# Fourier units of a hybrid GLA/FNet step: high and low data side by side in one moving operand

## The chip, the cores and the metric

The kernel runs on one core of a Trainium2 chip. Its engines work side by side, each through its own instructions in order: TensorE (PE; its weight loads are shown as PEld), VectorE (DVE), ScalarE (ACT), GpSimd (POOL) and SyncE (SP), which here issues the transfers. The metric is the device time of one execution in microseconds; the time given is the median of several runs.

## The reference

One layer of a diffusion backbone on 384 tokens (128 of context, 256 latent) of width 2048: modulation, a mixing sub-layer, a dense feed-forward sub-layer. The part that matters is the mixer's Fourier branch and the merge:

```python
fg = fo.astype(jnp.float32).reshape(bsz, t, FOURIER_GROUPS, FOURIER_GROUP_DIM)
f = jnp.fft.fft2(fg, axes=(1, 3), norm='ortho').real
...
gates = jax.nn.sigmoid(h @ lw['w_gate'] + lw['b_gate'])
g_a, g_b = jnp.split(gates, 2, axis=-1)
merged = g_a * (o @ lw['w_br_gla']) + g_b * (f @ lw['w_br_four'])
return merged @ lw['w_out'], s_f, s_b
```

All data are float32. Context and latent tokens are transformed separately, in 4 groups of 256 channels.

## The kernel before

**Precision and layout.** Activations lie transposed, channels on the 128 partitions and the 384 tokens in the free dimension. A float32 operand is kept as two float32r parts, high (the value rounded by a copy) and low (the difference), and a product is three products: high by high, high by low, low by high. `gemm` (L248) writes them in the order weight-high by data-high, weight-high by data-low, weight-low by data-high, each with its own weight load; PSUM sums them.

**The weight feed.** Weights come in tiles of 128 x 1024, in one fixed list `srcs`. `load` (L185) issues the next transfer from SP into one of two buffers `raw`. `split` (L205) makes the two parts: ACT casts `whi` (L218), DVE subtracts `wlo` (L219); there are four buffers of each. A tile of the Fourier projection is folded first (`fold`, L195): one addition and one subtraction on DVE (L199, L200) into the single buffer `ws`. `grab` (L239) takes the oldest finished tile and pushes the next one, so a tile is used three takes after its push. With `hold=True` the split of a folded tile is put off until `settle` (L228), which the unit calls at its end. PE, ACT, DVE and POOL run their instructions in the order in which the program writes them; SP is not in that list in this part, and its order is the framework's.

**The stage.** `dft` makes the transformed data: `eT` (cosine part) and `dT` (sine part), each four blocks of 128 channels by 194 columns. 194 is 65 + 129: of a real transform only half of the positions, and one more, are kept for context and latent tokens; the sum and the difference of the two parts give both halves. `pnr` holds one more row group (the Nyquist channels), multiplied by `wn`. Before the change the high parts of `eT` and `dT`, the low part of `eT` and `pnr` lie in one tile `edT` in the place C_lo, each block 194 columns (776 bytes) from the next, and the low part of `dT` is a tile `dlo` of its own.

**The order of the stage** is `mix_order` (L155): block o0, then for i = 1 to 7 the block o_i and the Fourier units b of 2i-2 and 2i-1; then a0, b14, a1, b15, a2 to a15. A block o is a projection with two weight tiles (48 products of 384 columns) whose result `gcol` (L967) turns into a gated, split `oT`: three transposes on PE, a SiLU on ACT, one DVE operation, a split. A block a is the GLA branch's projection (24 products of 384 columns), multiplied by its gate and added to what unit b of the same number has stored (L1018, L1019). `gate_of` (L950) loads the gate of a later block and applies the sigmoid on ACT. Pieces of another computation (`ada_rest`, on DVE) are interleaved at a fixed rate by blocks o and a.

**A Fourier unit** (`four`, L976) takes one folded tile, 512 columns for `eT` and 512 for `dT`, and makes 2 x 12 products of 194 columns and one with `wn` (L984) into one PSUM bank: the two halves of `pf`. ACT copies the second half to `fd` (L987), which has one buffer; DVE forms the 384 positions with two additions and two subtractions (L991, L992), multiplies by the gate (L995), SP stores the result to `four_d` (L996), and `settle` splits the held tile. PSUM has 3 buffers in the pool `psm` (where `pf` and the projections' results lie) and 5 in the pool `pss`.

Of the kernel before, what the change touches and what calls it, by code (L numbers as in the profile page):

```python
# [11 lines left out]
F32 = mybir.dt.float32  # L12
F32R = mybir.dt.float32r
# [7 lines left out]
P = 128  # L21
# [4 lines left out]
T = TC + TL  # L26
# [22 lines left out]
HT = HC + HL  # L49
# [47 lines left out]
def tile_step(ctx: ExitStack, tc: tile.TileContext, a, o):  # L97
    nc = tc.nc
    PE, ACT, DVE, POOL, SP = nc.tensor, nc.scalar, nc.vector, nc.gpsimd, nc.sync
# [3 lines left out]
    actp = ctx.enter_context(tc.tile_pool(name="actp", bufs=1))  # L103
# [124 lines left out]
    def settle():  # L228
        if half_done:
            half_done.pop()()  # L230

    def push(at=None, eng=DVE, hold=False):
        load()
        split(at, eng, hold)

    def take():
        return ready.pop(0)

    def grab(hold=False):  # L239
        w = take()  # L240
        push(hold=hold)
        return w
# [5 lines left out]
    def gemm(dst, w, x, kts, n=P, n0=0, k0=0, first=True, last=True):  # L248

        for k in range(kts):  # L250
            for j, (wi, xi) in enumerate(((0, 0), (0, 1), (1, 0))):
                PE.matmul(  # L252
                    dst, w[wi][:, k * n + n0 : k * n + n0 + P], x[xi][:, k0 + k, :],
                    start=first and k == 0 and j == 0, stop=last and k == kts - 1 and j == 2,
                )
# [21 lines left out]
    def split_act(hi, lo, src):  # L277
        ACT.copy(hi, src)
        DVE.tensor_sub(lo, src, hi.bitcast(F32))
# [29 lines left out]
    psm = ctx.enter_context(tc.tile_pool(name="psm", bufs=3, space=PSUM))  # L309
    pss = ctx.enter_context(tc.tile_pool(name="pss", bufs=5, space=PSUM))  # L310
    with ExitStack() as s:
# [95 lines left out]
        def xprod(u, kb, w):  # L407
            def mm():
                for j, (x_, w_) in enumerate(passes(w)):
                    PE.matmul(px, w_[:, u * P : (u + 1) * P], hT[x_][:, kb, :], start=j == 0, stop=j == 2)  # L410

            return mm, lambda dst=None: flush(xacc[u], kb == 0, dst)
# [127 lines left out]
        for t in range(3):  # L540
            vprod(KT - 1, prev[0], range(3), (t,))
            if t < XU:
                mm, fl = xprod(t, KT - 1, prev[1])
# [298 lines left out]
    with ExitStack() as s:  # L842
        pc = s.enter_context(tc.tile_pool(name="pc", bufs=1))
        fold_in.append(pc)
        b0 = C_CR
        cd = pc.tile([P, NC - b0], F32, name="cd")
        SP.dma_start(cd, a["consts"][:, b0:NC])
        oT = alloc_r("B", "o")

        cl = actp.tile([P, 13 * HT], F32R, tag="C_lo", name="edT").rearrange("p (n t) -> p n t", t=HT)  # L850
        eT, dT = (cl[:, 0:4], cl[:, 4:8]), (cl[:, 8:12], pc.tile([P, 4, HT], F32R, name="dlo"))
        pnr = cl[:, 12]
        fs = {}
        nyq = pc.tile([P, 3, P], F32, name="nyq")
        POOL.memset(nyq, 0.0)
# [2 lines left out]
        wn = pc.tile([P, D], F32R, name="wn")  # L858
        done = [0]

        def dft():


            def left(dst, stat, m):

                for lat, base, n in ((0, C_CT - b0, HC), (1, C_LT - b0, HL)):
                    for k in range(1 + lat):
                        c0 = base + (m * (1 + lat) + k) * n
                        PE.matmul(  # L869
                            dst[:, HC * lat : HC * lat + n], stat(lat + k), cd[:, c0 : c0 + n],  # L870
                            start=k == 0, stop=k == lat,
                        )

            for g in range(4):
                while done[0] < 2 * g + 2:
                    yield
                yield
                xc = pc.tile([P, 3, 2, 2, P], F32, tag="xc", name="xc")
                for t in range(3):
                    px = pss.tile([P, 257], F32, tag="side", name="px")  # L880
                    ts = slice(t * P, (t + 1) * P)
                    e, d = fs[g][:, 0, ts], fs[g][:, 1, ts]
                    PE.matmul(px, d, cd[:, 129:386], start=True, stop=False)  # L883
                    PE.matmul(px[:, 0:129], e, cd[:, 0:129], start=False, stop=True)

                    for m, c0 in enumerate((0, 129)):
                        ACT.copy(xc[:, t, m], px[:, c0 : c0 + P].unsqueeze(1).to_broadcast([P, 2, P]))
                    ACT.copy(nyq[:, t, g : g + 65 : 32], px[:, 128:129].to_broadcast([P, 3]))
                yield
                off = (P - 32 * g) % P  # L890
                rot = xc.rearrange("p t m r c -> p t m (r c)")
                for m, x in enumerate((eT, dT)):
                    pp = pss.tile([P, HT], F32, tag="side", name="pp")
                    left(pp, lambda k: rot[:, k, m, off : off + P], m)
                    split_act(x[0][:, g, :], x[1][:, g, :], pp)
                yield
            pn = pss.tile([P, HT], F32, tag="side", name="pn")
            left(pn, lambda k: nyq[:, k, :], 0)
            ACT.copy(pnr, pn)
            DVE.tensor_sub(pnr[64:96], pn[64:96], pnr[64:96].bitcast(F32))  # L900
            yield

        def nyq_weights():

            n = D // 2
            for h in range(2):
# [13 lines left out]
                yield  # L920

        df = dft()

        def side():
# [50 lines left out]

        def four(i):  # L976

            pf = psm.tile([P, 512], F32, tag="mm", name="pf")
            p = pf[:, 0 : 2 * HT].rearrange("p (m t) -> p m t", m=2)
            w = grab(hold=True)  # L980
            for m, x in enumerate((eT, dT)):
                gemm(p[:, m, :], [v[:, 512 * m : 512 * m + 512] for v in w], x, 4, last=m == 1)
                if m == 0:
                    PE.matmul(p[:, 0, :], wn[0:96, i * P : (i + 1) * P], pnr[0:96], start=False, stop=True)  # L984
            g, _ = gates.pop(("b", i))
            d = pc.tile([P, HT], F32, tag="fd", name="fd")
            ACT.copy(d, p[:, 1, :])  # L987
            y = pc.tile([P, T], F32, tag="yb", name="y", bufs=4)
            for lo, n, base in ((0, TC, 0), (TC, TL, HC)):
                h = n // 2  # L990
                DVE.tensor_add(y[:, lo : lo + h], p[:, 0, base : base + h], d[:, base : base + h])  # L991
                DVE.tensor_sub(  # L992
                    y[:, lo + h : lo + n], p[:, 0, base + h : base : -1], d[:, base + h : base : -1],
                )
            DVE.tensor_mul(y, y, g)  # L995
            SP.dma_start(four_d[i], y)  # L996
            settle()
# [3 lines left out]
        for b, i in mix_order:  # L1001
            if b == "o":
                if i == 1:
                    gate_of()
                proj(psm, hT, lambda p: gcol(p, i), sd)
                if i == 1:
                    gate_of()
                continue
            if b == "b":
                four(i)  # L1010
            else:
                if mT is None:
                    mT = alloc_A()
                    rate[0] = 0.15
                p = psm.tile([P, T], F32, tag="mm", name="pmm")
                gemm(p, grab(hold=True), oT, 8)
                g, y = gates.pop((b, i))
                DVE.tensor_mul(g, g, p)  # L1018
                DVE.tensor_add(y, y, g)  # L1019
                settle()  # L1020
                if late:
                    split_act(*late.pop())
                late.append((mT[0][:, i, :], mT[1][:, i, :], y))
                step(sd)
            gate_of()
# [6 lines left out]
    with ExitStack() as s:  # L1032
# [49 lines left out]
        for i in range(KT):  # L1082
            p = psm.tile([P, T], F32, tag="mm", name="pmm")
            for g in range(2):
                n = 2 * i + g - 2 * KT
                if n < -6:
                    w = grab()
                else:

                    w = take()  # L1090
# [132 lines left out]
        for k in range(KT + 1):  # L1223
# [9 lines left out]
            if k:  # L1233
                if k % 8 == 1:
                    hw = [take() for _ in range(HEAD)]
                for j, m in ((0, 0), (1, 0), (0, 1)):
                    for u in range(HEAD):
                        PE.matmul(  # L1238
                            hp[u], hw[u][j][:, ((k - 1) % 8) * P : ((k - 1) % 8 + 1) * P], h2[m][:, k - 1, :],
                            start=k == 1 and j == m == 0, stop=k == KT and m == 1,  # L1240
# [12 lines left out]
        pf = s.enter_context(tc.tile_pool(name="pf", bufs=1))  # L1253
# [75 lines left out]
        pairs = []  # L1329
# [75 lines left out]
        def grab2(kept=2):  # L1405
            w = take()
            while now:
                now.pop(0)()
            load_more(kept)
            split_next()  # L1410
            return w
# [52 lines left out]
        for u in range(HEAD):  # L1464
            kind, c, j = ffn_order[u]
            dst_of[kind](hp[u], c, j)
        n = 0
        for kind, c, j in ffn_order[HEAD:]:
            p = psm.tile([P, T], F32, tag="mm", name="pmm")
# [98 lines left out]
        for kind, c, i in steps:  # L1568
# [8 lines left out]
            if kind == "D":  # L1577
                w = grab2()
                n, kh = i // 2, i % 2
                if kh == 0:  # L1580
# [3 lines left out]
                    pool, tag = (pss, "side") if done % 2 or (c, n) == (NFC - 2, 3) else (psm, "mm")  # L1584
                    pd_tiles = [pool.tile([P, 512], F32, tag=tag, name="pdn") for _ in range(3)]
                    d_live[0] = 3
                h = hid_last if last_c else hid
# [27 lines left out]
            else:  # L1615
                if kind == "A" and i == 0:
                    banks(c)
                w = grab2()
# [18 lines left out]
        n = d_order[-1]  # L1637
# [144 lines left out]
```

## Time and profile before

| | |
|---|---|
| median of 3 runs | 1968.85 us (1968.83 to 1969.10) |
| the profiled execution | 1969.33 us, of which the span is 1967.6 us |
| granted TensorE clock | 0.999 |
| PE busy in the span | 99% |
| stage of the Fourier units (first to last product of a unit) | 598.66 to 705.1 us |
| products of the 16 units | 400, of 194 columns |
| DMA over the span | 380.08 MB, mean 193 GB/s |

How to read it. The page and the views give instructions by line, engine, operation and tile: `pf<-edT,whi` is a product that writes `pf` from `edT` and `whi`. In a timeline the columns are start (us), duration (us), engine, line, operation, tiles, shapes and the count of merged instructions; the brackets give the idle time of the engine before it and what released it. Products are pipelined, so the time from one start to the next, not the duration, is what a product costs. A row of the view by windows gives the window, its length, and for PE, PEld, DVE, ACT and POOL the busy time with the number of instructions, then the clock, the share of the DMA engines and GB/s. In the chain of waits a row is start, length, engine, tile, line and count. In the view of one tile three durations in ns (least, median, most) stand behind the count.

### The profile page before, as it was taken

Reading aid. Unit: us, or ns where it says so; the run is one execution under the profiler, and the core shown is the slowest. Engines: PE = TensorE matmul, PEld = TensorE weight load, DVE = VectorE, ACT = ScalarE, POOL = GpSimd, SP = SyncE. Lnnn points to the kernel's source line nnn. Section 1 sums busy time; section 2 is a strip of 40 time slices with the busy share of each in tenths; the row PEclk is TensorE's granted clock in tenths of the full one; section 3 lists DMA queues with packets and bytes.
Section 4 is the critical chain, followed back from the end, with each engine's and each line's share of the span. In section 5 each row is a group of like instructions: output and inputs, shape, how many; then the busy total and the mean of one; then the engine's idle time right before and its main releaser. Section 6 shows DMA issues by size and latency. Waiting matters only on the chain.

```text
span 1967.6 us, 27720 instructions
## 1 busy us (share of the span) xinstructions
PE 1951.9 (99%) x10704; PEld 1731.7 (88%) x10704; DVE 1620.2 (82%) x2043; ACT 905.7 (46%) x1265; POOL 32.2 (2%) x44
## 2 busy tenths in 40 slices
PE   8999999999999999999999999999999999999998
PEld 6779999999999999999988888888888888888886
DVE  5569788878767778877789998999898999887875
ACT  4233454544345645446454444444444444444444
POOL 0000000000000000004000000000000000000001
PEclk9999999999999999999999999999999999999999
DMA  9978677767755697655345445463636363626243
GB/s 388 372 257 275 211 255 238 234 218 246 238 183 182 197 312 222 196 171 203 119 136 186 149 140 162 154 188 118 193 127 205 100 209 103 208 75 193 75 161 128
DMA packets 189412, 380.08 MB, mean 193 GB/s; under 512 B 14172, under 2 KB 112668, under 8 KB 184928
## 3 DMA queue, kind: packets, MB, share of 16 engines
q1 hardware_dynamic: 189136, 377.92, 59.0%
q8 instruction: 84, 1.38, 0.3%
q14 instruction: 48, 0.39, 0.1%
q10 hardware_dynamic: 144, 0.39, 0.1%
HBM read 361.48 MB, written 16.78 MB: 192 GB/s over the span
## 4 chain that ended last, share of the span: by engine, by line
PE 96%; DMA 1%; DVE 1%; ACT 1%; issue 0%; SPq 0%; POOL 0%; DVEq 0%; ACTq 0%; POOLq 0%
PE pmm L252 35%; PE pgu L1484 30%; PE pdn L1484 18%; PE pv L392 3%; PE pf L252 2%; PE pgm L375 1%; DMA slab<-in_w_ada 1%; PE px L410 1%; PE pmm L1238 1%; PE ptr L1545 1%; PE po L639 1%; DMA raw<-in_w_d 0%; PE pr L574 0%; PE dl L639 0%; PE pp L869 0%; PE px L883 0%
## 5 line engine op out<-in xcount | busy, mean ns | idle before, releaser
L252 PE MATMUL pmm<-A_hi,whi 128*128 128x384 f32 x1200 | 404.2, 337 | 0.0
L252 PE MATMUL pmm<-A_hi,wlo 128*128 128x384 f32 x1200 | 401.3, 334 | 0.0
L252 PE MATMUL pmm<-A_lo,whi 128*128 128x384 f32 x1200 | 401.2, 334 | 0.0
L1385 ACT CAST whi<-u 128x1024 fp32r<-128x1024 f32 x200 | 210.6, 1053 | 275.7 <-DVE u L1369 86.2
L1385 ACT CAST whi<-raw 128x1024 fp32r<-128x1024 f32 x175 | 184.2, 1053 | 209.7 <-DMA raw<-in_w_g 69.8
L218 ACT CAST whi<-raw 128x1024 fp32r<-128x1024 f32 x181 | 189.9, 1052 | 182.4 <-DMA raw<-in_w_gate 59.6
L219 DVE TENSOR_TENSOR wlo<-raw,whi 128x1024 fp32r<-128x1024 f32 x179 | 218.0, 1222 | 66.9 <-ACT whi L218 66.5
L1396 DVE TENSOR_TENSOR wlo<-u,whi 128x1024 fp32r<-128x1024 f32 x200 | 244.2, 1221 | 29.3 <-ACT whi L1385 16.7
L1484 PE MATMUL pgu<-whi,A_hi 128*128 128x512 f32 x640 | 250.0, 391 | 0.0
L1484 PE MATMUL pgu<-whi,A_lo 128*128 128x512 f32 x640 | 249.3, 389 | 0.0
L1396 DVE TENSOR_TENSOR wlo<-raw,whi 128x1024 fp32r<-128x1024 f32 x175 | 213.5, 1220 | 32.3 <-ACT whi L1385 22.7
L252 PEld LDWEIGHTS pmm<-A_hi,whi 128*128 128x128 f32 x1200 | 225.3, 188 | 2.5 <-issue 1.4
L252 PEld LDWEIGHTS pmm<-A_lo,whi 128*128 128x128 f32 x1200 | 225.4, 188 | 0.2
L252 PEld LDWEIGHTS pmm<-A_hi,wlo 128*128 128x128 f32 x1200 | 225.3, 188 | 0.0
L566 DVE SCALAR_TENSOR_TENSOR adacc<-adaw,spad,adacc 128x1024 f32<-128x1024 f32 x180 | 222.8, 1279 | 1.0 <-DMA adaw<-in_w_ada 0.7
L1484 PE MATMUL pdn<-whi,hid_hi 128*128 128x512 f32 x480 | 186.9, 389 | 0.0
L1484 PE MATMUL pdn<-whi,hid_lo 128*128 128x512 f32 x480 | 186.8, 389 | 0.0
L1484 PE MATMUL pgu<-wlo,A_hi 128*128 128x512 f32 x640 | 184.2, 389 | 0.0
L1484 PEld LDWEIGHTS pgu<-whi,A_hi 128*128 128x128 f32 x640 | 120.1, 188 | 26.1 <-issue 0.8
L1484 PEld LDWEIGHTS pgu<-wlo,A_hi 128*128 128x128 f32 x640 | 120.1, 188 | 25.4
L1484 PEld LDWEIGHTS pgu<-whi,A_lo 128*128 128x128 f32 x640 | 120.2, 188 | 25.0
L1484 PE MATMUL pgu<-whi,S 128*128 128x512 f32 x480 | 131.1, 395 | 0.0
(363 smaller groups left out, 2790.2 us busy)
## 6 DMA issues: line engine op xcount, KB each, us to landing
adaw<-in_w_ada SPq DMA_DIRECT2D x96, 512.0 KB, 4.2
raw<-in_w_d SPq DMA_DIRECT2D x88, 512.0 KB, 3.8
slab<-in_w_ada SPq DMA_DIRECT2D x32, 1024.0 KB
raw<-in_w_gate SPq DMA_DIRECT2D x64, 512.0 KB, 4.6
raw<-in_w_g SPq DMA_DIRECT2D x48, 512.0 KB, 3.7
raw<-in_w_u SPq DMA_DIRECT2D x48, 512.0 KB, 4.3
raw<-in_w_in SPq DMA_DIRECT2D x44, 512.0 KB, 3.7
u<-in_w_u SPq DMA_DIRECT2D x40, 512.0 KB, 4.9
```

The lines of the kernel that those rows point to most:

```text
L218: ACT.copy(hi, raw)
L219: sub = lambda: eng.tensor_sub(lo, raw, hi.bitcast(F32))
L252: PE.matmul(dst, w[wi][:, k * n + n0 : k * n + n0 + P], x[xi][:, k0 + k, :], start=first and k == 0 and j == 0, stop=last and k == kts - 1 ...
L375: PE.matmul(pgv[q : q + 32, :], spad[:, k, :], slab[k // (KT // 2)][:, k % (KT // 2), :], start=k < 4, stop=k >= KT - 4,)
L392: PE.matmul(pv[2 * t + g], hT[x_][:, kb, t * P : (t + 1) * P], w_[:, g * 512 : (g + 1) * 512], start=kb == 0 and j == 0, stop=kb == KT - 1 ...
L410: PE.matmul(px, w_[:, u * P : (u + 1) * P], hT[x_][:, kb, :], start=j == 0, stop=j == 2)
L566: DVE.scalar_tensor_tensor(acc[:, c, :], w, spad[:, k, c : c + 1], acc[:, c, :], op0=ALU.mult, op1=ALU.add,)
L639: PE.matmul(dst, w[wi], x[xi], start=first and j == 0, stop=last and j == 2)
L1238: PE.matmul(hp[u], hw[u][j][:, ((k - 1) % 8) * P : ((k - 1) % 8 + 1) * P], h2[m][:, k - 1, :], start=k == 1 and j == m == 0, stop=k == KT ...
L1385: ACT.copy(hi, src)
L1396: DVE.tensor_sub(lo, src, hi.bitcast(F32))
L1484: PE.matmul(dst, stat[x_][m], mov(w[w_], m), start=first and w_ == m == x_ == 0, stop=last and w_ == m == 1,)
```

## The change

High and low part of a block of `eT` or `dT` now lie side by side: a pair of 2 x 194 = 388 columns. Eight pairs, 448 columns (1792 bytes) from start to start, lie in two buffers: six and `pnr` in the place C_lo, two in a new tile `d2` at the head of the pool `pc`; the tile `dlo` is gone. In a unit, per block, one product of weight-high with the whole pair (388 columns) takes the place of two of 194, and weight-low with the high part stays a product of 194. The two products with weight-high thus end in two ranges of columns. `eT` and `dT` get a PSUM bank each, the one in `psm`, the other in `pss`. For each of them ACT copies the high-by-low range to `d` (which has now two halves) and DVE adds the other range from PSUM; the four operations that form `y` then read `d` alone. The order of the unit's other work is kept. 25 products a unit become 17; ACT has 2 copies in place of 1; DVE has 2 additions more.

```diff
+        pw = 448
+        d2 = pc.tile([P, 2 * pw], F32R, name="d2")
...
-        cl = actp.tile([P, 13 * HT], F32R, tag="C_lo", name="edT").rearrange("p (n t) -> p n t", t=HT)
-        eT, dT = (cl[:, 0:4], cl[:, 4:8]), (cl[:, 8:12], pc.tile([P, 4, HT], F32R, name="dlo"))
-        pnr = cl[:, 12]
+        cl = actp.tile([P, 6 * pw + HT], F32R, tag="C_lo", name="edT")
+        pairs = [x[:, n * pw : n * pw + 2 * HT] for x, k in ((cl, 6), (d2, 2)) for n in range(k)]
+        eT, dT = pairs[:4], pairs[4:]
+        pnr = cl[:, 6 * pw :]
...
-                    split_act(x[0][:, g, :], x[1][:, g, :], pp)
+                    split_act(x[g][:, 0:HT], x[g][:, HT:], pp)
...
         def four(i):
-            pf = psm.tile([P, 512], F32, tag="mm", name="pf")
-            p = pf[:, 0 : 2 * HT].rearrange("p (m t) -> p m t", m=2)
             w = grab(hold=True)
+            d = pc.tile([P, 2, HT], F32, tag="fd", name="fd")
+            y = pc.tile([P, T], F32, tag="yb", name="y", bufs=4)
             for m, x in enumerate((eT, dT)):
-                gemm(p[:, m, :], [v[:, 512 * m : 512 * m + 512] for v in w], x, 4, last=m == 1)
+                pf = (pss if m else psm).tile([P, 512], F32, tag="side" if m else "mm", name="pf")
+                for k in range(4):
+                    c = slice(512 * m + k * P, 512 * m + (k + 1) * P)
+                    PE.matmul(pf[:, 0 : 2 * HT], w[0][:, c], x[k], start=k == 0, stop=False)
+                    PE.matmul(pf[:, 0:HT], w[1][:, c], x[k][:, 0:HT], start=False, stop=m == 1 and k == 3)
                 if m == 0:
-                    PE.matmul(p[:, 0, :], wn[0:96, i * P : (i + 1) * P], pnr[0:96], start=False, stop=True)
+                    PE.matmul(pf[:, 0:HT], wn[0:96, i * P : (i + 1) * P], pnr[0:96], start=False, stop=True)
+                ACT.copy(d[:, m], pf[:, HT : 2 * HT])
+                DVE.tensor_add(d[:, m], d[:, m], pf[:, 0:HT])
             g, _ = gates.pop(("b", i))
-            d = pc.tile([P, HT], F32, tag="fd", name="fd")
-            ACT.copy(d, p[:, 1, :])
-            y = pc.tile([P, T], F32, tag="yb", name="y", bufs=4)
             for lo, n, base in ((0, TC, 0), (TC, TL, HC)):
                 h = n // 2
-                DVE.tensor_add(y[:, lo : lo + h], p[:, 0, base : base + h], d[:, base : base + h])
+                DVE.tensor_add(y[:, lo : lo + h], d[:, 0, base : base + h], d[:, 1, base : base + h])
                 DVE.tensor_sub(
-                    y[:, lo + h : lo + n], p[:, 0, base + h : base : -1], d[:, base + h : base : -1],
+                    y[:, lo + h : lo + n], d[:, 0, base + h : base : -1], d[:, 1, base + h : base : -1],
                 )
             DVE.tensor_mul(y, y, g)
             SP.dma_start(four_d[i], y)
```

## The prediction

> **What bounds the kernel now.** I read the page's engine table and its chain of waits first, then the stage of the Fourier units (598 to 706 us) by windows, then that stage's timeline engine by engine.
>
> ```profile
> PE 1951.9 (99%) x10704; PEld 1731.7 (88%) x10704; DVE 1620.2 (82%) x2043; ACT 905.7 (46%) x1265; POOL 32.2 (2%) x44
> 627.14:641.38 14.24, 14.24 (x104) 14.20 (x103) 11.18 (x21) 9.41 (x13) 0.00 (x0) 1.00 0.71 207
> ```
>
> The second row is one turn of the stage in the view by windows: one projection column block ("o", two weight tiles) and two Fourier units ("b", one tile each). TensorE (PE) is busy all 14.24 us, its weight loads 14.20, VectorE (DVE) 11.18, ScalarE (ACT) 9.41, at the full clock. Read alone, this says that a shorter PE is a shorter kernel. The question is what else goes round in nearly the same time.
>
> Every weight tile is loaded (SP), split into a high part by ACT and a low part by DVE, and used three takes later. One turn of that feed, from the first "raw" cast of a turn to the next one (timeline, rows of ACT, DVE and SP, most others left out):
>
> ```profile
> 626.61 1.05 ACT L218 CAST whi<-raw 128x1024 fp32r<-128x1024 f32 x1 [0.45 <-DMA raw<-in_w_in]
> 630.57 1.05 ACT L218 CAST whi<-raw 128x1024 fp32r<-128x1024 f32 x1
> 631.52 0.31 ACT L987 COPY fd<-pf 128x194 f32<-128x194 f32 x1
> 631.65 1.22 DVE L219 TENSOR_TENSOR wlo<-raw,whi 128x1024 fp32r<-128x1024 f32 x1 [0.40 <-ACT whi L218]
> 632.79 0.22 DVE L991 TENSOR_TENSOR y<-pf,fd 128x64 f32<-128x64 f32 x1
> ...
> 633.25 0.28 DVE L992 TENSOR_TENSOR y<-pf,fd 128x128 f32<-128x128 f32 x1
> 633.57 0.56 DVE L995 TENSOR_TENSOR y<-y,gate 128x384 f32<-128x384 f32 x1
> 634.05 0.68 DVE L199 TENSOR_TENSOR ws<-raw 128x512 f32<-128x512 f32 x1
> 634.65 0.68 DVE L200 TENSOR_TENSOR ws<-raw 128x512 f32<-128x512 f32 x1
> 635.36 0.33 SPq L190 DMA_DIRECT2D raw<-in_w_in  x1
> 638.37 0.69 DVE L200 TENSOR_TENSOR ws<-raw 128x512 f32<-128x512 f32 x1
> 639.09 1.05 ACT L218 CAST whi<-ws 128x1024 fp32r<-128x1024 f32 x1 [2.24 <-DVE ws L200]
> 640.58 1.05 ACT L218 CAST whi<-raw 128x1024 fp32r<-128x1024 f32 x1 [0.45 <-DMA raw<-in_w_in]
> ```
>
> Nothing in this ring waits for PE. The cast at 626.61 starts the gate, its products and the second cast; DVE then does wlo, the first unit's y group, the fold, the second unit's y group, wlo and the second fold (ends 639.06), ACT casts that tile, and the next turn begins at 640.58. It takes 13.97 us, only 0.27 less than PE's turn. Two paths close it: the engines' own order (13.97 less the 0.45 that the cast waits = 13.52), and the transfer that the first fold frees (issued 635.36, landed 640.58). The other turns begin here; the bracket is what ACT waited for the transfer:
>
> ```profile
> 612.64 1.05 ACT L218 CAST whi<-raw 128x1024 fp32r<-128x1024 f32 x1 [0.77 <-DMA raw<-in_w_in]
> 655.37 1.05 ACT L218 CAST whi<-raw 128x1024 fp32r<-128x1024 f32 x1 [1.28 <-DMA raw<-in_w_in]
> 669.97 1.05 ACT L218 CAST whi<-raw 128x1024 fp32r<-128x1024 f32 x1 [0.82 <-DMA raw<-in_w_in]
> 684.34 1.05 ACT L218 CAST whi<-raw 128x1024 fp32r<-128x1024 f32 x1 [0.85 <-DMA raw<-in_w_br_gla]
> ```
>
> How far the feed is ahead is read from the end of a tile's low part (DVE) and the first product that uses it (PE):
>
> ```profile
> 683.52 1.23 DVE L219 TENSOR_TENSOR wlo<-ws,whi 128x1024 fp32r<-128x1024 f32 x1 [1.12 <-ACT whi L218]
> 688.60 0.28 PE L252 MATMUL pf<-edT,wlo 128*128 128x194 f32 x1
> 693.25 1.22 DVE L219 TENSOR_TENSOR wlo<-ws,whi 128x1024 fp32r<-128x1024 f32 x1
> 695.56 0.28 PE L252 MATMUL pf<-edT,wlo 128*128 128x194 f32 x1
> 700.78 1.22 DVE L219 TENSOR_TENSOR wlo<-ws,whi 128x1024 fp32r<-128x1024 f32 x1
> 702.51 0.28 PE L252 MATMUL pf<-edT,wlo 128*128 128x194 f32 x1
> 704.45 0.22 DVE L991 TENSOR_TENSOR y<-pf,fd 128x64 f32<-128x64 f32 x1
> 705.34 0.41 PE L252 MATMUL pmm<-o_hi,whi 128*128 128x384 f32 x1
> ```
>
> Unit 13 has 3.85 us in hand, unit 14 has 695.56 - 694.47 = 1.09, unit 15 has 702.51 - 702.00 = 0.51. So in the last turns the feed is as good as the bound already.
>
> **The change part by part.** *PE: 25 products of 194 columns become 8 of 388 and 9 of 194.*
>
> ```profile
> 601.52 0.39 PE L252 MATMUL pf<-edT,whi 128*128 128x194 f32 x2
> 604.31 0.36 PE L252 MATMUL pmm<-A_hi,whi 128*128 128x384 f32 x1
> 604.51 0.34 PE L252 MATMUL pmm<-A_lo,whi 128*128 128x384 f32 x1
> 604.22 0.19 PEld L252 LDWEIGHTS pmm<-A_hi,whi 128*128 128x128 f32 x1
> 604.33 0.19 PEld L252 LDWEIGHTS pmm<-A_lo,whi 128*128 128x128 f32 x1
> 705.34 162.51 PE pmm L252 x936
> 1028.48 5.44 PE pgu L1484 x24
> ```
>
> One unit runs from 601.52 to 604.31: 2.79 us, 112 ns a product. 384 columns take 162.51/936 = 174 ns, 512 take 5.44/24 = 227, so 0.415 ns a column: 388 columns 175, and 194 would take 95. They take 112 because weight loads start 0.11 apart (604.22, 604.33): a short product is bound by the load behind it. A long one hides its successor's load, the short one after it does not: a pair is 175 + 112 = 287 ns against 3 x 112 = 335. A unit is 8 x 287 + 112 = 2.41 us, 0.38 less; 16 units, 6.1 us. This order of widths isn't in the trace. From below, 8 x (175 + 95) + 112 = 2.27 a unit, if the load hid entirely; from above, each long product behind a short one takes 0.20 as at 604.31, 25 ns more: 2.61. PE's gain is 2.9 to 8.3 us; I take 6.1, the load interval being the nearest row.
>
> *Addresses.* The pairs, 1792 bytes apart, and the two buffers' places change no instruction. No row before has a moving operand whose place could be told to matter, so I cost it at 0; from above, a long product at the price of two weight loads (223 ns) makes a unit 2.79 again.
>
> *ACT and DVE: one copy and two additions more a unit.* Each half of the data now leaves PSUM as high plus low: ACT copies one, DVE adds the other.
>
> ```profile
> L279 DVE TENSOR_TENSOR edT<-pp,edT x4: 353/359/359, 529.0 to 590.1; 128x194 fp32r<-128x194 f32 x4
> L1018 DVE TENSOR_TENSOR gate<-gate,pmm x16: 546/547/550, 699.6 to 765.1; 128x384 f32<-128x384 f32 x16
> L995 DVE TENSOR_TENSOR y<-y,gate x16: 557/558/560, 605.2 to 711.7; 128x384 f32<-128x384 f32 x16
> ```
>
> An addition of this size with one operand in PSUM is 0.359 us. Behind each other, operations overlap 0.08 (634.05 + 0.68 to 634.65); the first y needs the second sum, so it loses that overlap and gains the gap of 0.04 (633.25 + 0.28 to 633.57). Per unit, e = 2 x 0.276 + 0.12 = 0.67 us of DVE, ahead of y. The y group now reads SBUF alone; at 384 columns that is 558 ns against 547 with one operand in PSUM, so nothing is saved. From below, e = 0.55 (no dependence gap); from above, 0.84 (no overlap at all). ACT's copy of 0.31 lies beside this: ACT waits 2.24 us a turn for the second fold, and its copies at 631.52 precede DVE's use by a microsecond. Without that cover it would cost 0.31.
>
> [...]
>
> *Who waits for it.* Behind the additions in DVE's order stand y, the fold and the next tile's wlo; behind these the cast on ACT, SP's next load, and PE. In a turn the engines' path grows by 2e (two units), the transfer's path by e (only the first unit's sums stand before the fold that frees the tile). The turn grows by the greater of 2e less the bracket, and e less r, where r is what the transfer gains because the store and the gate load of the second unit are issued e later; r lies between 0 and 0.67, and I take the middle.
>
> Lateness against the rows above: 612.64, one unit before it: 0.67. 626.61 and 640.58: 1.34 - 0.45 = 0.89 each. 655.37: 1.34 - 1.28 = 0.06, or the transfer's 0.34. 669.97: 0.52. 684.34: 0.49. Together 3.80 us. Unit 14's tile has unit 12's sums before it: 4.47 late, 1.09 in hand. Unit 15's tile has unit 13's too: 5.14 late, 0.51 in hand, so its first low product starts 4.63 later, at 707.14. From there the new unit needs 2.41 - 0.175 = 2.23, so the block after it starts at 709.37 in place of 705.34: **4.0 us later**. A second gate there agrees: that block takes the PSUM buffer of unit 14, freed by its first sum at 704.45 + 4.47 + 0.36, and 0.15 for the hand-over: 709.43. PE's 6.1 us turn into waiting; behind this point PE has work without a gap (162.51 us of it), so nothing is given back.
>
> The profiled run took 1969.33 us (span 1967.6), 0.48 above the median; 1973.3 for it, **1972.8** against the median of 1968.85.
>
> **The rivals.** *PE stays the bound, faster.* Place: every unit; price: 6.1 us, 1962.8. It decides if DVE's 0.67 falls into DVE's idle time, 14.24 - 11.18 = 3.06 a turn. For it: PE's full row. Against: that idle time lies inside the ring (DVE waiting for the cast), and 1.09 and 0.51 us in hand can't take 14 units of it. Chance 0.12. [...]
>
> [...] Chance 0.16. [...]
>
> *The sums wait for their copies, slower still.* The copies' buffer is one, so an odd unit's copies wait for the even unit's y; if DVE then waits copy by copy, a sum takes about twice as long (0.67 rather than 0.33) in half the units, e is 1.0, and the end 8 us later: 1976.9. Against: the fold's 1.28 us lie between. Chance 0.12.
>
> *It doesn't shorten PE* (223 ns for a long product): the end is still the feed's, unit 15 is 0.38 longer: 1973.2, within the forecast.
>
> **How the numbers follow.** The forecast has 0.60; with e = 0.55 and the transfer fully relieved it is 2.4 us later, with e = 0.84 and no relief 6.4: 1971.2 to 1975.2. A difference from no change can be told from 0.2%, 3.9 us (1972.8), so two thirds of it, 0.40, count as slower, 0.20 as no change. With the rivals: faster 0.12, same 0.36, slower 0.52. The range 1968.5 to 1977.0 leaves out the faster rival and half of the slowest.
>
> **What would show it.** Right: products of 388 columns 175 ns apart and units of 2.41 us where PE doesn't wait; turns of the "raw" cast of 14.6 to 14.9 us; PE idle ahead of the units, above all 14 and 15, put down to DVE's wlo or ACT's whi; the long run of 936 products starting at about 709.4. Wrong: turns still near 14.0, or no idle time on PE in this stage (then the kernel is faster).

## The result, and the profile after

| | before | after |
|---|---|---|
| median of 18 runs, us | 1968.93 (1968.80 to 1969.88) | 1972.82 (1972.31 to 1973.93) |
| ratio of the two | | 1.0020, 95% interval 1.0013 to 1.0027 |
| profiled run, us (its span) | 1969.33 (1967.6) | 1972.35 (1970.6) |
| shortest turn of the feed, raw cast to raw cast, us | 13.97 | 14.81 |
| the same, mean of five turns, us | 14.34 | 14.87 |

The changed kernel is 0.2% slower: 3.89 us by the medians. The two profiled runs differ by 3.02, because that of before lies 0.40 above its median and that of after 0.47 below.

The engine table of the changed kernel, and its chain of waits by engine (shares of the span):

```profile
PE 1949.7 (99%) x10576; PEld 1727.3 (88%) x10576; DVE 1629.0 (83%) x2075; ACT 908.9 (46%) x1281; POOL 32.2 (2%) x44
PE 93%; DVE 3%; ACT 2%; DMA 1%; issue 1%; SPq 0%; POOL 0%; DVEq 0%; ACTq 0%; POOLq 0%
```

PE has 128 products fewer and DVE 32 operations more, which are the two sums of 16 units. The rest of the table looks as before; the 0.2% doesn't show in shares of the span. It shows in the stage. Two turns by windows, each from one raw cast to the next (sum, then busy time of PE, its weight loads, DVE, ACT, POOL; clock; DMA share; GB/s):

```profile
627.92:642.73 14.81, 14.00 (x89) 13.64 (x87) 12.11 (x24) 9.49 (x15) 0.00 (x0) 1.00 0.63 196
642.73:657.54 14.81, 13.99 (x95) 12.80 (x94) 12.10 (x24) 9.50 (x16) 0.00 (x0) 1.00 0.61 194
```

PE was busy for the whole of its turn of 14.24 us before. Now the turn is 14.81 and PE stands idle for 0.8 of it, at the full clock. The loss is larger than this idle time: two units without a wait take 4.88 us in place of 5.65, so PE by itself would need 13.47 and loses 1.34 a turn. (In part because a product of 388 columns is followed after 0.20 us in a row, but counts as busy for its whole 0.44 us ahead of a wait.) DVE has 12.1 us of work where it had 11.2. The transfers move less per microsecond than before (194 to 196 GB/s against 207).

The six turns begin here (timeline, ACT's raw casts; a bracket would say what ACT waited for):

```profile
613.10 1.05 ACT L218 CAST whi<-raw 128x1024 fp32r<-128x1024 f32 x1
...
627.92 1.04 ACT L218 CAST whi<-raw 128x1024 fp32r<-128x1024 f32 x1
...
642.73 1.04 ACT L218 CAST whi<-raw 128x1024 fp32r<-128x1024 f32 x1
...
657.54 1.05 ACT L218 CAST whi<-raw 128x1024 fp32r<-128x1024 f32 x1
...
672.63 1.04 ACT L218 CAST whi<-raw 128x1024 fp32r<-128x1024 f32 x1
...
687.44 1.04 ACT L218 CAST whi<-raw 128x1024 fp32r<-128x1024 f32 x1
```

Turns of 14.82, 14.81, 14.81, 15.09 and 14.81 us. Before, these casts had brackets of 0.45 to 1.28 us for a transfer. Now none has one: the transfer is always there first, and the engines' own order sets the turn alone. So the mean turn grew by 0.53 us only, while the engines' part of it grew by 1.3 (from 13.52 to 14.81). What grew in that order is seen on DVE (one unit, from its sums to the fold of the next tile):

```profile
648.90 0.61 DVE L995 TENSOR_TENSOR fd<-fd,pf 128x194 f32<-128x194 f32 x2
649.55 0.22 DVE L999 TENSOR_TENSOR y<-fd 128x64 f32<-128x64 f32 x1
...
650.03 0.28 DVE L1000 TENSOR_TENSOR y<-fd 128x128 f32<-128x128 f32 x1
650.35 0.56 DVE L1003 TENSOR_TENSOR y<-y,gate 128x384 f32<-128x384 f32 x1
650.83 0.68 DVE L199 TENSOR_TENSOR ws<-raw 128x512 f32<-128x512 f32 x1
```

From the first operation of the unit's group to the fold it is 650.83 - 648.90 = 1.93 us. Before, it was 634.05 - 632.79 = 1.26. The difference is 0.67.

PE's waits from 598 to 712 us (total, times, longest):

```profile
PEld pf L991 <- DVE wlo L219: 6.3, 6, 1.7
PE pf L991 <- DVE wlo L219: 4.7, 5, 1.5
...
PE pf L990 <- ACT whi L218: 0.8, 1, 0.8
```

PE waits for the low part of a unit's weight tile, five times for 4.7 us, and once for a high part. (The first row is the weight load of the same products, which waits beside them.) The end of the stage, from the timeline of PE and DVE:

```profile
696.36 0.45 PE L990 MATMUL pf<-edT,whi 128*128 128x388 f32 x1 [0.82 <-ACT whi L218]
...
697.01 1.22 DVE L219 TENSOR_TENSOR wlo<-ws,whi 128x1024 fp32r<-128x1024 f32 x1
...
698.28 0.36 PE L991 MATMUL pf<-edT,wlo 128*128 128x194 f32 x1 [1.48 <-DVE wlo L219]
...
699.64 0.58 PE L990 MATMUL pf<-edT,whi 128*128 128x388 f32 x1
700.02 0.37 PE L991 MATMUL pf<-edT,wlo 128*128 128x194 f32 x1
...
704.63 1.23 DVE L219 TENSOR_TENSOR wlo<-ws,whi 128x1024 fp32r<-128x1024 f32 x1
...
708.78 0.36 PE L252 MATMUL pmm<-o_hi,whi 128*128 128x384 f32 x1
```

Unit 14's low part ends at 698.23 and its first use starts 0.05 later: nothing is in hand any more. Behind the two waits of 0.82 and 1.48 us the products of 388 columns take 0.38 us each from start to start (699.64 to 700.02), against 0.20 at the full clock (601.20 to 601.40, shown further down); the granted clock says why:

```profile
696.30:698.28 1.98, 0.45 (x1) 0.19 (x1) 1.89 (x3) 1.95 (x4) 0.00 (x0) 1.00 0.85 297
...
699.27:702.20 2.93, 2.93 (x13) 2.93 (x13) 2.86 (x9) 0.67 (x3) 0.00 (x0) 0.50 0.90 315
702.20:703.50 1.30, 1.30 (x8) 1.30 (x7) 1.30 (x4) 0.00 (x0) 0.00 (x0) 0.83 0.99 351
```

The granted clock is 0.50 for 2.93 us and 0.83 on average for 1.30: 2.93 x 0.50 + 1.30 x 0.17 = 1.7 us of PE time are gone. The next block starts at 708.78 against 705.34, 3.44 us late, and PE has work without a gap from there. To be 3.44 us late in spite of a gain of 6.1, PE must have lost 9.5 us: 5.5 are the waits listed above and 1.7 the clock; the rest, 2.3, fits the loss at the waits that the profile doesn't count as idle (four turns with 0.5 each), an estimate.

### The profile page after: what moved, and what is told of

The parts are those of the page before. It is cut to its first block, busy times and chain, and to the rows that moved or that the text cites. A ratio compares the mean times of both kernels' runs of the same rounds, so it can differ in the third digit from the quotient of the medians.

```text
span 1970.6 us, 27516 instructions
## 1 busy us (share of the span) xinstructions
PE 1949.7 (99%) x10576; PEld 1727.3 (88%) x10576; DVE 1629.0 (83%) x2075; ACT 908.9 (46%) x1281; POOL 32.2 (2%) x44
## 4 chain that ended last, share of the span: by engine, by line
PE 93%; DVE 3%; ACT 2%; DMA 1%; issue 1%; SPq 0%; POOL 0%; DVEq 0%; ACTq 0%; POOLq 0%
PE pmm L252 33%; PE pgu L1492 30%; PE pdn L1492 18%; PE pv L392 3%; PE pgm L375 1%; DMA slab<-in_w_ada 1%; PE px L410 1%; PE pmm L1246 1%; PE ptr L1553 1%; PE pf L990 1%; DVE wlo L219 1%; ACT whi L218 1%; PE po L639 1%; DMA raw<-in_w_d 0%; PE pf L991 0%
```

## The experiments

The theory, called "feed" below: the two sums stand in DVE's order ahead of the next fold and low part, so the ring that feeds the weights turns in 14.8 us, and PE's shorter units become waiting. The rivals: the wide products or their addresses cost the time; ACT's second copy does; DVE's total work does, whatever its order; SP's queue does. Each was tried by itself, SP's queue only in part. All times are medians in microseconds, each with the kernel before in runs on the same chip. The changed kernel's 1972.82 is from the runs of the result, not from these; the kernel before lies between 1968.93 and 1969.18 in all of them.

| run | this | before | ratio, 95% interval |
|---|---|---|---|
| epilogue alone | 1973.46 | 1969.18 | 1.0025 (1.0015 to 1.0035) |
| products alone | 1969.11 | 1969.18 | 0.9999 (0.9990 to 1.0008) |
| second copy, no sums | 1968.36 | 1969.18 | 0.9996 (0.9987 to 1.0005) |
| sums twice | 1981.76 | 1969.18 | 1.0066 (1.0052 to 1.0080) |
| pairs packed | 1972.85 | 1969.02 | 1.0018 (1.0010 to 1.0027) |
| first half wide | 1972.11 | 1969.00 | 1.0014 (1.0005 to 1.0023) |
| units spread | 1967.93 | 1969.02 | 0.9989 (0.9980 to 0.9998) |
| before, units spread | 1968.98 | 1969.02 | 1.0000 (0.9991 to 1.0009) |
| gate product later | 1965.43 | 1969.00 | 0.9982 (0.9973 to 0.9991) |
| before, gate product later | 1968.94 | 1969.00 | 0.9999 (0.9990 to 1.0008) |
| spread and later | 1966.59 | 1969.00 | 0.9990 (0.9981 to 0.9999) |
| store later | 1972.82 | 1969.02 | 1.0020 (1.0010 to 1.0029) |

**The epilogue alone.** Products of 194 columns, as before, under the copies and sums of the change:

```diff
-                    PE.matmul(pf[:, 0 : 2 * HT], w[0][:, c], x[k], start=k == 0, stop=False)
+                    PE.matmul(pf[:, 0:HT], w[0][:, c], x[k][:, 0:HT], start=k == 0, stop=False)
+                    PE.matmul(pf[:, HT : 2 * HT], w[0][:, c], x[k][:, HT:], start=False, stop=False)
```

> Every product stays 194 columns wide (high by low goes into the second range by products of its own), but the second copy and the two sums of the changed kernel are there. Leaves nothing out. Theory 'feed': the longer way of VectorE per unit (0.67 us) makes the turn of the feed 14.8 us whatever the products do; PE's own turn is about 14.2 us, so the end comes 3 to 4.5 us after that of the kernel before: 1972 to 1973.5 us, as the changed kernel. Theory 'products' (the wide products or their addresses cost the time): 1968.9 us, as before. Theory 'both': 1970.5 to 1971.

Two raw casts of its timeline, and the longest of PE's waits:

```profile
642.83 1.05 ACT L218 CAST whi<-raw 128x1024 fp32r<-128x1024 f32 x1
...
657.66 1.05 ACT L218 CAST whi<-raw 128x1024 fp32r<-128x1024 f32 x1
```

```profile
PE pf L992 <- DVE wlo L219: 1.9, 2, 1.5
```

The turn is 14.83 us, as in the changed kernel, and the whole loss is there (4.3 us) without a single wide product. PE, whose turn is longer here, waits for the feed only at the last two units.

**The products alone.** The wide products, under the epilogue of before:

```diff
-                ACT.copy(d[:, m], pf[:, HT : 2 * HT])
-                DVE.tensor_add(d[:, m], d[:, m], pf[:, 0:HT])
+                if m == 0:
+                    p0 = pf
+                else:
+                    ACT.copy(d[:, 1], pf[:, 0:HT])
...
-                DVE.tensor_add(y[:, lo : lo + h], d[:, 0, base : base + h], d[:, 1, base : base + h])
+                DVE.tensor_add(y[:, lo : lo + h], p0[:, base : base + h], d[:, 1, base : base + h])
```

> The products of the changed kernel (388 columns, pairs 1792 bytes apart), with the epilogue of the kernel before, which reads the first 194 columns of each range; the product of the high weights with the low data is computed but not added. Theory 'feed': the turn of the feed goes back to about 14.0 us, PE's to about 13.5 us, so the feed still sets the turns; 1968.0 to 1968.9 us, within 1 us of the kernel before. Theory 'products': 1972 us or more. A PE that is the bound of the turns would give 1968.9 - 6.1 = 1962.8 us.

No loss, and no gain either (0.2 us above the range), although two units take 4.88 us where PE doesn't wait, as in the changed kernel, against 5.65 before. The brackets of before are back on the raw casts:

```profile
626.84 1.05 ACT L218 CAST whi<-raw 128x1024 fp32r<-128x1024 f32 x1 [0.98 <-DMA raw<-in_w_in]
...
641.16 1.05 ACT L218 CAST whi<-raw 128x1024 fp32r<-128x1024 f32 x1 [0.79 <-DMA raw<-in_w_in]
```

The turns between the six raw casts are 14.2 us on average (14.34 before), 0.2 more than expected, while PE could do one in 13.5: a PE that is 6 us faster lands on the feed as it was. It runs ahead until the feed's lead is used up, then waits 1.40 and 0.86 us for unit 14's tile and loses 1.7 us more by a halved clock behind these waits (0.50 from 694 to 697 us; see the last section). What little lead is left (the block behind unit 15 starts at 704.31, before 705.34) goes in the next blocks. The last pieces of this run's chain of waits there:

```profile
722.35 9.23 DMA raw<-in_w_br_gla
731.68 1.07 ACT whi L218
...
734.60 133.39 PE pmm L252 x768
```

The next blocks' weights are late too: one tile takes 9.23 us to come. Behind that PE runs without a wait, 0.15 us off the kernel before at 867.9 us.

**The second copy without the sums.**

```diff
-                ACT.copy(d[:, m], pf[:, HT : 2 * HT])
-                DVE.tensor_add(d[:, m], d[:, m], pf[:, 0:HT])
+                ACT.copy(d[:, m], pf[:, 0:HT])
```

> The changed kernel with both copies of ScalarE (of the first 194 columns of each range) and without the two sums; the product of the high weights with the low data is computed but not added. Theory 'feed by the sums': turn about 14.0 us, 1968.0 to 1969 us. Theory 'feed by the copies' (ScalarE's casts come later by a second copy of 0.32 us per unit): 1971 to 1973 us.

1968.36: the second copy costs nothing that can be measured, as it lies in ACT's waits (2.24 us a turn for the second fold before the change, and the copy takes 0.31).

**The sums twice.**

```diff
                 DVE.tensor_add(d[:, m], d[:, m], pf[:, 0:HT])
+                DVE.tensor_add(d2x[:, m], d[:, m], pf[:, 0:HT])
```

> The changed kernel with each of the two sums done twice (the second one into a tile that nobody reads); leaves nothing out. Theory 'feed by the sums': 2 x 0.35 us more per unit, so the turn of the feed goes from 14.81 to about 16.2 us and the end moves by 5 to 7 turns x 1.4 us: 1979 to 1983 us. Theory 'products' or 'copies': VectorE is busy 83% and has room, 1972.8 to 1973.5 us.

DVE's rows, from the first sum to y, and PE's waits:

```profile
636.95 0.35 DVE L996 TENSOR_TENSOR fd<-fd,pf 128x194 f32<-128x194 f32 x1
...
638.27 0.22 DVE L1001 TENSOR_TENSOR y<-fd 128x64 f32<-128x64 f32 x1
```

```profile
PE pf L992 <- DVE wlo L219: 11.3, 11, 2.1
```

Four sums take 638.27 - 636.95 = 1.32 us where two took 0.65. The turn is 16.14 us (raw casts at 614.64, 630.78 and 646.92), 1.33 more than with two: twice 0.67. The run is 8.9 us slower than the changed kernel. So the loss follows the sums, and each microsecond of them in a turn is paid at every turn.

**The pairs packed.** `pw = 388` in place of 448: pairs 1552 bytes apart, nothing else.

> The changed kernel with the pairs 388 elements (1552 bytes) apart instead of 448 (1792 bytes): only the addresses differ; leaves nothing out. Theory 'feed': 1972.8 us, as the changed kernel, and turns of 14.81 us. Theory 'addresses' (the distance of 1792 bytes is what costs, or what saves): at least 2 us away from 1972.8 to either side, and a wide product followed by a narrow one takes another time than 287 ns.

1972.85, turns of 14.82: the distance of the pairs does nothing.

**The first half wide.** The change for m = 0 alone: one sum and one copy fewer.

> The change for the first half of each unit alone (m = 0 with products of 388 columns and a sum; m = 1 with three products of 194 columns into one range and one copy); leaves nothing out. Theory 'feed': one sum instead of two, so the turn of the feed is 14.81 - 2 x 0.33 = 14.15 us, PE's 13.86: 1968.8 to 1970.5 us. If the loss comes with any second copy or any wide product: 1972 us or more.

A miss: 1972.11, above the range, and in the range of the rival (any second copy or any wide product). The runs with the products alone and with the second copy have both without a loss, so that rival falls all the same. DVE's rows:

```profile
633.37 0.35 DVE L1000 TENSOR_TENSOR fd<-fd,pf 128x194 f32<-128x194 f32 x1
633.81 0.23 DVE L1006 TENSOR_TENSOR y<-fd 128x64 f32<-128x64 f32 x1
```

One sum costs 0.44 us (633.81 - 633.37), not half of 0.67: the gap before y, which needs the sum's result, comes once with one sum or with two. (It is 0.09 us here and 0.04 behind two sums; why isn't known.) The first three turns are 14.35 us on average (raw casts at 612.81 and 655.87), 0.83 over the engines' path of before (13.52), 0.42 a unit. That explains 0.2 us a turn; the profiled run lost further time in the blocks behind the units (it is 0.4 us behind the kernel before at 705.7 and 1.7 behind at 869.5) and in the last stage, where PE waits 0.95 and 0.54 us for DVE's `hidE` (an operand of the last products) in place of 0.43. Why these fell out worse than in the runs above wasn't settled.

**The units spread.** If the feed's lead runs out because two units come in a row, another order of blocks should help:

```diff
+    nb = 0
...
-        mix_order += [("o", i), ("b", 2 * i - 2), ("b", 2 * i - 1)]
-    mix_order += [("a", 0), ("b", 14), ("a", 1), ("b", 15)] + [("a", i) for i in range(2, KT)]
+        mix_order.append(("o", i))
+        for _ in range(2 - i % 2):
+            mix_order.append(("b", nb))
+            nb += 1
+    for i in range(KT):
+        mix_order.append(("a", i))
+        if i % 2 == 0 and nb < KT:
+            mix_order.append(("b", nb))
+            nb += 1
```

> The changed kernel with another order of the blocks: behind the output blocks one unit and two units in turn (o0, o1 b0, o2 b1 b2, o3 b3, o4 b4 b5, o5 b5.. up to o7 b9), and the last seven units one behind every second block a; leaves nothing out. Theory 'feed': a unit asks the feed and VectorE for two pieces in a short time on PE, a block for two pieces in a long one, so fewer units in a row leave the feed its lead, PE waits less, and PE's gain of 6 us shows: 1963 to 1967 us. If the feed's total over the whole stretch is the bound and not its lead at the units: 1971.5 to 1973.5 us.

> The kernel before with the same order of blocks as the run with the units spread; leaves nothing out. Theory 'feed': there PE already sets the turns, nothing to gain: 1968.4 to 1969.2 us. If the order by itself gives the gain: 1966 us or less.

A miss by 0.9 us for the first, though in the direction of the theory: on the changed kernel the order gives 4.9 us (1967.93), on the kernel before nothing (1968.98). So a part of the wide products' gain shows that the feed had hidden. It is not the whole: at 867 us the profiled run, 1.6 us faster than the median of its kernel, is 3.15 us ahead of the kernel before, not 6.

**The gate's product later.** The sums stay, and another operation leaves the chain: the product of y with the gate, and the store behind it, wait until DVE has an idle stretch, behind the folds of the next output block.

```diff
+    def flush_muls():
+        while muls:
+            muls.pop(0)()
...
                 ACT.copy(hi, raw)
+                if pairs and not hold:
+                    flush_muls()
                 sub = lambda: eng.tensor_sub(lo, raw, hi.bitcast(F32))
...
-            DVE.tensor_mul(y, y, g)
-            SP.dma_start(four_d[i], y)
             settle()
+
+            def mul():
+                DVE.tensor_mul(y, y, g)
+                SP.dma_start(four_d[i], y)
+
+            muls.append(mul)
```

(The gates have five buffers in place of four, and in the second stage the products go behind the next grab.)

> The changed kernel, in which VectorE's product of a unit with its gate (0.48 us) and the store of the unit are put off: not behind the unit's y, but into the 1.17 us in which VectorE waits for the cast behind the folds of the next output block (in the second stage behind the next grab). Leaves nothing out. Theory 'feed': the sums cost because they stand in VectorE's chain ahead of the next fold; two products of 0.48 us taken out of that chain bring the turn from 14.81 to about 13.9 us, as without the sums (13.9 to 14.0 by the run of the products alone), and the end to 1967.5 to 1969.5 us. If VectorE's total work is what counts, and not its order: 1972.3 to 1973.2 us, as the changed kernel.

> The kernel before with the gate's product put off; leaves nothing out. Theory 'feed': its turns are set by PE (14.24 us), so nothing is gained: 1968.5 to 1969.3 us. If the later product gives a gain by itself: 1967.5 us or less.

The first is a miss on the fast side of its range, 1965.43: 7.4 us less than the changed kernel and 3.6 less than the kernel before, which doesn't profit from the same step (1968.94). One turn by windows, then DVE's rows:

```profile
625.56:639.19 13.63, 13.63 (x90) 13.59 (x88) 11.92 (x24) 9.52 (x16) 0.00 (x0) 1.00 0.72 213
```

```profile
632.86 0.28 DVE L1006 TENSOR_TENSOR y<-fd 128x128 f32<-128x128 f32 x1
633.06 0.68 DVE L199 TENSOR_TENSOR ws<-raw 128x512 f32<-128x512 f32 x1
...
637.46 0.69 DVE L200 TENSOR_TENSOR ws<-raw 128x512 f32<-128x512 f32 x1
638.06 1.02 DVE L1012 TENSOR_TENSOR y<-y,gate 128x384 f32<-128x384 f32 x2
639.32 1.23 DVE L225 TENSOR_TENSOR wlo<-ws,whi 128x1024 fp32r<-128x1024 f32 x1 [0.24 <-ACT whi L222]
```

In the changed kernel DVE waited here for ACT's cast:

```profile
642.86 1.23 DVE L219 TENSOR_TENSOR wlo<-ws,whi 128x1024 fp32r<-128x1024 f32 x1 [1.17 <-ACT whi L218]
```

Both products of a turn now lie in that wait; of its 1.17 us, 0.24 is left. The turn is 13.63 us and PE is busy in all of it. It shrank by 1.18, more than the two products' 0.96: in the changed kernel the product waits 0.04 for y's result (650.03 + 0.28 to 650.35), while the fold, which needs nothing of y, overlaps y's end by 0.08 here (632.86 + 0.28 to 633.06). The long run of the blocks starts at 701.4 against 705.34, so 4.0 of PE's 6.1 us show; the rest is in PE's waits around the last two units (1.6 us) and in the turn, which is still 0.16 above PE's own (13.47).

DVE's work is the same as in the changed kernel but for its order. So the rival "DVE's total work" falls.

**The store later.** In that run the store had moved too, and it stands in SP's queue ahead of a raw load. The store alone, at the same place (and with the five gate buffers of that run):

> The changed kernel in which the gate's product stays where it was and the store of the unit alone is put off, to the place it had in the run with the gate's product later; leaves nothing out. In that run two things moved at once: VectorE's product left the chain ahead of the next fold, and the store, which waits for it in SyncE's queue with the next raw load behind it, went behind that load. Theory 'VectorE's chain': the changed kernel's casts wait for no load, so the store alone gains nothing: turns of 14.8 us, 1972.0 to 1973.3 us. Theory 'SyncE's queue': turns below 14.3 us and 1970.5 us or less.

1972.82, turns of 14.81: nothing gained. SP's waits from 612 to 684 us show a limit of this run:

```profile
SPq L1013 <- DVE y L1009: 13.6, 9, 1.5
```

The store still made SP wait there (14.0 us in the changed kernel), so SP's queue was not emptied. What speaks against the queue as the cause is that none of the six raw casts of the changed kernel shown above waits for a transfer.

**Spread and later.** Both steps together.

> The order of blocks of the run with the units spread, and the gate's product put off as in the run before this one; leaves nothing out. Theory 'feed': the waits of 0.4 to 0.7 us that are left before single units in the second stage shrink too: 1964 to 1967.5 us, the fastest of all. If those waits come from elsewhere (transfers, casts): 1967.5 to 1968.5 us, as with the units spread alone.

1966.59, in the range and slower than the later product alone. The waits before units have gone, and others have come, before blocks of the second stage (PE's waits):

```profile
PE pmm L266 <- DVE gate L1047: 1.6, 2, 1.1
```

A block waits for its PSUM buffer, which DVE frees by the product with the gate. Units between these blocks give DVE more to do just there; that this is the cause was not tested.

## Why the prediction was right, and where not

- **PE's units.** 2.41 us was right, and so was the sum of a pair, but not its parts. The changed kernel's timeline:

```profile
601.20 0.36 PE L990 MATMUL pf<-edT,whi 128*128 128x388 f32 x1
601.40 0.25 PE L991 MATMUL pf<-edT,wlo 128*128 128x194 f32 x1
601.49 0.36 PE L990 MATMUL pf<-edT,whi 128*128 128x388 f32 x1
```

  A pair takes 0.29 us from 601.20 to 601.49 (287 ns predicted), split into 0.20 for the wide product and 0.09 for the narrow one, not 175 and 112. The wide product pays what the narrow one was to pay: two errors in the parts that cancel.
- **The sums.** e = 0.67 us a unit was measured to the hundredth, with the gap before y that the first-half run shows by itself.
- **The turn.** The prediction compares one turn of each loop, 13.97 of the feed with 14.24 of PE. Over the five turns that it lists, the feed's mean is 14.34 (684.34 - 612.64, over 5) and PE's 14.52 (the first products of the units at 612.91 and 685.52, over 5): as near to each other as it says. The engines' path was to become 13.52 + 2 x 0.67 = 14.86 us; it is 14.81. The transfer's path was to bind in part of the turns; it dropped out of all of them. That is the term that was most mis-sized: r, the relief of the transfer, was taken at its middle and was all there. The turn from 642.73 to 657.54 is 0.02 us longer than before, not 0.34. The first turn began 0.46 late, not 0.67; why isn't known. Lateness at the last raw cast is 687.44 - 684.34 = 3.10, not 3.80.
- **Units 14 and 15.** Unit 14's low part came 3.76 late, not 4.47, the same 0.7 less, and took all that was in hand, as predicted. Unit 15's low part was to be the last one that PE waits for. It came 3.85 late (704.63 against 700.78), not 5.14, and PE didn't wait for it:

```profile
706.57 0.25 PE L991 MATMUL pf<-edT,wlo 128*128 128x194 f32 x1
```

  That is 0.71 us behind the low part's end (705.86). PE itself was late by then, as the clock had halved after the waits at unit 14. An estimate without that loss: PE would have waited for unit 15 until 705.86 and started the block 2.23 later, at 708.09, 2.75 us late. So of the 3.44 us, 2.75 are the feed and 0.7 the clock; the forecast of 4.0 had 4.0 of the feed and no clock. Two errors of opposite sign made the end come out near. That the median agrees to 0.02 us is luck: the profiled run was to take 1973.3 us and took 1972.35, and the two medians differ by 0.9 more than the two profiled runs.
- **Given back?** At 867 us the delay is still 3.4 us, as predicted; in the last stage 0.4 of it goes: PE's wait of 0.43 us there, for DVE's `hidE`, is gone.
- **What was costed at nothing.** ACT's second copy, the addresses and the buffers' places: nothing, by the runs with the copy, the packed pairs and the products alone. The clock had no term in the sum, and the waits cost 1.7 us of PE time by it.
- **The rivals.** PE as the bound: the run with the products alone has PE's whole gain and ends where the kernel before does. PE is the busiest engine (99%), and a faster PE gave nothing that can be told there (1969.11 against 1969.18 us); in the changed kernel two products a turn moved on an engine that is busy 83% gave 7.4. Cheap sums: the chance of 0.16, which is in the 0.36 for the same time, was for sums that cost little, and no run shows such a cost: they took 0.67 us a unit, and y's 128-column operations take 0.28 us whether one operand is in PSUM (before) or none is (after), so reading SBUF alone saved nothing there. Sums that wait for their copies: both sums run together in 0.61 us, so no.

## What to carry to other kernels

When two loops turn in nearly the same time, making one shorter shows nothing until the other is (14.34 and 14.52 us a turn before the change; with PE's shorter units alone the kernel took 1969.11 against 1969.18); cost a change by what it adds to the loop that closes last, at every turn, and not by the busy shares. In an engine's order, only what stands between two steps of that loop is paid for: the same sums cost 3.9 us with the gate's product behind them, and with that product moved into an idle stretch the wide products gained 3.6 over the kernel before. An operation's cost in such a chain includes the gap before whoever needs its result, and here that gap didn't halve when the operations did: from the first sum to y, two sums took 0.65 us with a gap of 0.04 before y, one 0.44 with a gap of 0.09.

## What the hardware showed that was not expected

- Behind two short waits of PE close to each other the granted clock was halved. In the changed kernel 0.82 and 1.48 us of idle time within 3 us, with one product between them, were followed by a granted clock of 0.50 for about 3 us. A clock of 0.50 came too behind 1.40 and 0.86 us (products alone), 1.51 and 0.88 (second copy), 0.84 and 1.48 (pairs packed), 0.84 and 1.49 (store later) and 0.85 and 2.14 (sums twice). It stayed at 1.00 behind 0.50 and 1.46 (epilogue alone) and 0.59 and 1.32 (first half wide). So the runs with the halved clock had 2.26 us or more of idle time in the two waits, the others 1.96 or less. No run was made to test that it is the sum that counts.
- In a row of pairs a product of 388 columns took 0.20 us and the one of 194 behind it 0.09 (601.20, 601.40 and 601.49 in the changed kernel), less than the 0.11 between the narrow products of a unit before (2.79 us for 25).
